# Column fixes on GpSimd, four spectra kept, and the last 16 projections written behind the second filter's forward products

## The chip, the cores and the metric

The kernel runs on one NeuronCore of a Trainium2 chip. The core has five engines that work at the same time, each through its own list of instructions in order: TensorE (matrix products, PE in the profile, with its weight loads as PEld), VectorE (DVE), ScalarE (ACT), GpSimd (POOL) and SyncE (SP), which here only issues transfers. ScalarE and GpSimd issue transfers too; all of them run on 16 DMA engines. The metric is the device time of one execution in microseconds (us), as the median of several.

## The reference

One residual layer of a sequence model, 1024 time steps by 1024 channels, in float32. After an RMS norm one projection gives 56 blocks of 128 columns: inputs and gates of a state-space branch, three inputs and a gate of a Hyena branch, and merge gates. The change touches only the Hyena branch. Cut to what matters:

```python
sc = conv_b
for j in range(3):                      # width-3 convolution in time of the projections
    sc = sc + pp[:, j:j + L] * conv_w[j]
v, x1, x2 = jnp.split(sc, 3, axis=-1)
kf = hyena_filters(...)                 # spectra of two filters, length 2L
z = v
for o, g in enumerate((x1, x2)):
    zf = jnp.fft.rfft(z, n=2 * L, axis=1)
    conv = jnp.fft.irfft(zf * kf[:, o][None], n=2 * L, axis=1)[:, :L]
    z = g * (conv + d[o] * z)
return z * jax.nn.silu(gate)
...
merged = m[..., :D] * y_s5 + m[..., D:] * (y_hy @ w_branch_hy)
out = rmsnorm(x + merged @ w_out)
```

So there are two rounds of forward transform, product with a filter's spectrum, and way back (inverse transform and gate). The second round needs the first one's result; its gate x2 times silu(gate) needs only the projections.

## The kernel before

**Projections.** `proj(c, use)` computes one block of 128 columns for all 1024 time steps: 48 products of 128x512 into a PSUM tile `pps` of two banks, in three passes of 16 (high part of the weights with the high and the low part of x, low part of the weights with the high part of x). `use` then reads the tile away. There are two `pps` tiles. A weight block is loaded by SyncE (`wraw`), ScalarE writes its high part `whi` and the negative of that into `wlo`, and a transfer issued by GpSimd adds `wraw` to `wlo` (line 512); there are two pairs of `whi` and `wlo` and three `wraw`.

**Forward transforms** (`forward`). For a group of 256 channels, products with constant matrices `zc` (3 MB in SBUF) give even parts `fwe` and odd parts `fwo` in four PSUM tiles. There are 4 groups of 4 steps each. VectorE joins even and odd parts, multiplies with the filter's spectrum `kt` (lines 718 and 719) and forms the result, which ScalarE's queue stores to memory (`d_y`). Two steps take 39 products.

**Ways back** (`inverse`). One of 8 channel blocks takes four spectra `yraw`, which ScalarE and VectorE split into high and low parts `y`, and 48 products with the constants `ic` into one PSUM tile `iv`. ScalarE copies half of it (`isn`), VectorE forms sum and difference (`pm`). In the first way back (`hy_inverse0`, `rotate`), GpSimd multiplies with the gate and writes sum and difference back into the gate's tile, and two VectorE instructions repair the first column (lines 823 and 824). Then eight transposes (`zt`) turn it, and it is stored for the second round. There are five gate tiles, three of them named `gate`, two inside `u`.

**The second forward stage** (`hy_forward1`) runs a generator of the forward steps and, in a loop over 8 blocks, two projections each: the silu gate, and x2 with its convolution and product with that gate (`fold`, lines 588 to 590: half of the product on GpSimd, half on VectorE). After each projection the loop lets some steps through, by a table:

```python
for _ in range((2, 3, 0)[(2 * c + i) % 3]):
    next(f, None)
```

After the twelfth projection it closes the stage's pools, so that the SBUF of the forward constants goes to the constants and buffers of the second way back (`inverse_tail`). That way back runs together with the first two projections of the branch's output (`w_branch_hy`); six more, and the product with `w_out`, follow.

**What sets the order.** The kernel is written in a framework that builds each engine's list ahead of the run: an instruction's place in the program is its priority, and the builder takes a later instruction first where it reckons that an earlier one must wait. It also hands out buffers, and adds the waits on semaphores. At run time each engine keeps to its list.

**Where tiles lie.** The forward constants of the second stage lie where the gate tiles lay, so their load waits for the last transposes of the first way back. The constants of the second way back lie where the second stage's buffers lay.

Of the kernel before, what the change touches and what calls it, by code (L numbers as in the profile page):

```python
# [12 lines left out]
ALU = mybir.AluOpType  # L13
# [87 lines left out]
class Trunk:  # L101
# [703 lines left out]
    def hy_inverse0(self):  # L805

        tc, nc = self.tc, self.nc
        self.d_z1 = self.dram.tile([4, 128, 2, 2048], F, name="d_z1")
        with ExitStack() as ctx:
            self.inv_pools(ctx, 0, (4, 2))  # L810
            zp = ctx.enter_context(tc.tile_pool(name="iv_z", bufs=1, side="right"))
            pi = ctx.enter_context(tc.tile_pool(name="iv_p", bufs=1, space=PSUM, side="right"))
            pt = ctx.enter_context(tc.tile_pool(name="iv_pt", bufs=2, space=PSUM, side="right"))
            gates, back = {}, {}
            self.inverse_start(0)

            def rotate(c):
                g = gates.pop(c)
                pm = self.inverse(pi)
                nc.gpsimd.tensor_tensor(out=pm, in0=pm, in1=g, op=ALU.mult)  # L820
                nc.gpsimd.tensor_tensor(out=g[:, 0], in0=pm[:, 0], in1=pm[:, 1], op=ALU.add)
                nc.gpsimd.tensor_tensor(out=g[:, 1], in0=pm[:, 0], in1=pm[:, 1], op=ALU.subtract)
                nc.vector.tensor_copy(out=g[:, 0, 0:1], in_=pm[:, 0, 0:1])
                nc.vector.tensor_scalar(out=g[:, 1, 0:1], in0=pm[:, 1, 0:1], scalar1=-1.0, scalar2=None, op0=ALU.mult)
                back[c] = g

            def store(c):
                z = zp.tile([128, 2, 8, 128], R, name="z1")
                self.to_time(pt, back.pop(c).rearrange("p a b -> p (a b)"), z)
                nc.scalar.dma_start(out=self.d_z1[c // 2][:, c % 2], in_=z.rearrange("p h a c -> p (h a c)").bitcast(F))  # L830

            for c in range(10):
                def use_x1(ps):
                    g = self.gates[c % len(self.gates)]
                    self.fold(self.conv(ps, 8 + c, "cv"), None, g)
                    gates[c] = g.rearrange("p a b c d -> p a (b c d)")

                if c < 8:
                    self.proj(16 + c, use_x1)
                if 0 < c < 9:  # L840
                    rotate(c - 1)
                if c > 1:
                    store(c - 2)

    def hy_forward1(self, tail):

        nc = self.nc
        self.d_x2 = self.dram.tile([8, 128, L], F, name="d_x2")
        with self.tc.tile_pool(name="sg", bufs=1) as sp, self.tc.tile_pool(name="vf1", bufs=2) as self.vf, \
                ExitStack() as ctx:  # L850
            wp, fwd = self.fwd_pools(ctx, 1)

            def forwards():
                for cq in range(4):
                    z = wp.tile([128, 2, 2, 8, 128], R, name="z")
                    for ct in range(2):
                        nc.sync.dma_start(out=z[:, ct].rearrange("p h a c -> p (h a c)").bitcast(F),
                                          in_=self.d_z1[cq][:, ct])
                    yield
                    yield from fwd(cq, z)  # L860

            f = forwards()
            next(f)
            for c in range(8):
                silu = sp.tile([128, L], F, name="sg")

                def use_g(ps):
                    nc.scalar.activation(out=silu, in_=ps, func=AF.Silu)

                def use_x2(ps):  # L870
                    t = self.vf.tile([128, 2, 2, 2, 128], F, name="vf")
                    self.fold(self.conv(ps, 16 + c, "cv"), silu, t)
                    nc.scalar.dma_start(out=self.d_x2[c], in_=t.rearrange("p a b c d -> p (a b c d)"))

                for i, (col, use) in enumerate(((32 + c, use_g), (24 + c, use_x2))):
                    self.proj(col, use)
                    for _ in range((2, 3, 0)[(2 * c + i) % 3]):
                        next(f, None)
                    if 2 * c + i == 11:
                        ctx.close()  # L880
                        tail()

    def exp(self, pool, out, x, shape):

# [598 lines left out]
```

## Time and profile before

| | |
|---|---|
| median of 3 runs | 1446.65 us (1445.04 to 1446.68) |
| the profiled execution | 1447.77 us |
| its span, from the first to the last instruction | 1445.9 us |
| around the span | 1.87 us |
| TensorE busy in the span | 93% |
| VectorE busy in the span | 70% |
| mean granted TensorE clock | 0.972 of 2.4 GHz |

The share of busy time is a mean over stages with different limits. A wait is worth something only where TensorE, or what it will wait for, ends last. Matmuls overlap each other, so the time of one is read from a long run of them, not from its own duration.

### The profile page before, as it was taken

The page shows a single profiled execution, that of the slowest core. Times are in us where ns is not written, and L with a number is a line of the kernel's source. Part 1 is how long each engine was busy: PE and PEld are TensorE (multiplying, and loading weights), DVE is VectorE, ACT ScalarE, POOL GpSimd, SP SyncE. Part 2 cuts the span into 40 slices and gives each one's busy share as a digit, 9 for nine tenths or more (in the row PEclk, how much of TensorE's full clock was granted, in tenths as well). Part 3 has the DMA queues.
Part 4 walks back from the last instruction along what each step waited for, and adds up shares of the span by engine and source line. Part 5 has one row for each costly group of instructions (what it writes and reads, how often), then busy time and mean ns, then how long its engine had stood idle before and what let it go on. Part 6 is the DMA issues. An engine that isn't in the chain of part 4 may idle for free.

```text
span 1445.9 us, 19569 instructions
## 1 busy us (share of the span) xinstructions
PE 1343.9 (93%) x7219; PEld 1132.4 (78%) x7219; DVE 1009.2 (70%) x1954; ACT 515.7 (36%) x737; POOL 379.6 (26%) x315
## 2 busy tenths in 40 slices
PE   5888999999999999999999999999999925999998
PEld 3776898888888887878788888888888825978886
DVE  7999997698689877224399994554379984842632
ACT  5576663223233332442322322533322213422322
POOL 3766774000000000232112100343311111432222
PEclk9998999999999999999999999999999967999999
DMA  8211225855784654667956569767788889666332
GB/s 277 90 73 73 89 110 144 199 154 140 201 264 109 139 127 84 167 159 223 315 162 172 178 175 282 195 175 200 254 265 267 268 253 306 184 175 160 119 115 73
DMA packets 188618, 257.23 MB, mean 178 GB/s; under 512 B 23069, under 2 KB 144153, under 8 KB 185788
## 3 DMA queue, kind: packets, MB, share of 16 engines
q1 hardware_dynamic: 149212, 153.69, 34.2%
q0 software_dynamic: 11520, 39.85, 14.6%
q10 hardware_dynamic: 27792, 62.45, 12.1%
q8 instruction: 57, 0.93, 0.3%
q14 instruction: 37, 0.30, 0.1%
HBM read 147.49 MB, written 76.82 MB: 155 GB/s over the span
## 4 chain that ended last, share of the span: by engine, by line
PE 66%; DVE 14%; DMA 8%; issue 2%; ACTq 0%; ACT 0%; SPq 0%; DVEq 0%
PE pps L541 42%; PE iv L634 6%; PE ops L1384 6%; DMA d_y<-x 3%; PE po L404 2%; DMA zc<-c_zc_lo_d 2%; PE fwo L685 2%; PE pe L414 1%; PE fwe L685 1%; DVE st L1216 1%; PE zt L670 1%; DVE st L1214 1%; PE s5ps L1166 1%; DVE e L338 1%; DVE m L719 1%
## 5 line engine op out<-in xcount | busy, mean ns | idle before, releaser
L512 POOL DMA_DIRECT2D wlo<-wraw x76 | 66.8, 879 | 717.8 <-ACT wlo L511 568.3
L541 PE MATMUL pps<-xh,whi 128*128 128x512 f32 x896 | 229.1, 400 | 3.2 <-DVE cv L565 3.2
L541 PE MATMUL pps<-xl,whi 128*128 128x512 f32 x896 | 224.3, 397 | 0.0
L541 PE MATMUL pps<-xh,wlo 128*128 128x512 f32 x896 | 223.9, 396 | 0.0
L541 PEld LDWEIGHTS pps<-xh,whi 128*128 128x128 f32 x896 | 165.9, 189 | 40.1 <-ACT wlo L511 3.6
L541 PEld LDWEIGHTS pps<-xh,wlo 128*128 128x128 f32 x896 | 166.5, 188 | 38.3
L541 PEld LDWEIGHTS pps<-xl,whi 128*128 128x128 f32 x896 | 166.2, 188 | 38.2 <-issue 0.2
L510 ACT CAST whi<-wraw 128x1024 fp32r<-128x1024 f32 (+1 forms) x76 | 74.7, 983 | 310.3 <-PE pps L541 267.9
L404 PE MATMUL po<-sh,fo 128*128 128x256 f32 x512 | 99.8, 289 | 6.9 <-DVE sh L111 5.7
L634 PEld LDWEIGHTS iv<-ic,y 128*128 128x128 f32 x752 | 96.3, 193 | 3.3 <-DVE y L113 0.6
L634 PE MATMUL iv<-ic,y 128*128 128x256 f32 (+1 forms) x752 | 97.7, 285 | 0.0
L113 DVE TENSOR_TENSOR y<-yraw,y 128x512 fp32r<-128x512 f32 x64 | 52.8, 837 | 55.4 <-ACT y L109 54.9
L404 PEld LDWEIGHTS po<-sh,fo 128*128 128x128 f32 x512 | 82.8, 194 | 9.8 <-DVE sh L111 6.7
L511 ACT ACTIVATE wlo<-whi 128x1024 fp32r<-128x1024 f32 (+1 forms) x76 | 74.9, 985 | 20.6 <-PE pps L541 20.4
L357 POOL TENSOR_TENSOR acc<-acc,sq 128x512 f32<-128x512 f32 x56 | 76.4, 1365 | 21.7 <-ACT sq L342 20.0
L404 PE MATMUL po<-sl,fo 128*128 128x256 f32 x256 | 73.4, 287 | 1.0 <-DVE sl L113 1.0
L109 ACT CAST y<-yraw 128x512 fp32r<-128x512 f32 x64 | 39.2, 620 | 76.2 <-PE iv L634 45.9
L563 DVE SCALAR_TENSOR_TENSOR cv<-pps,cw,cv 128x1023 f32<-128x1023 f32 x24 | 30.7, 1280 | 30.4 <-ACT cv L562 30.4
L685 PE MATMUL fwo<-z,zc 128*128 128x256 f32 x384 | 51.7, 288 | 0.0
L404 PEld LDWEIGHTS po<-sl,fo 128*128 128x128 f32 x256 | 49.5, 193 | 2.3 <-DVE sl L113 1.6
L685 PEld LDWEIGHTS fwo<-z,zc 128*128 128x128 f32 x384 | 50.1, 197 | 1.0
L333 PE MATMUL g<-w3h,ha 128*128 128x512 f32 x64 | 32.6, 510 | 18.4 <-DVE e L338 16.6
(437 smaller groups left out, 2662.4 us busy)
## 6 DMA issues: line engine op xcount, KB each, us to landing
wlo<-wraw POOLq DMA_DIRECT2D x64, 512.0 KB, 5.8
wraw<-w_in SPq DMA_DIRECT2D x56, 512.0 KB, 4.7
kspec<-ko SPq DMA_DIRECT2D x32, 512.0 KB, 3.0
kt<-kspec SPq DMA_DIRECT2D x32, 512.0 KB, 5.4
d_y<-x ACTq DMA_DIRECT2D x32, 512.0 KB, 3.9
yraw<-d_y SPq DMA_DIRECT2D x64, 256.0 KB, 4.9
d_m<-cv ACTq DMA_DIRECT2D x16, 512.0 KB, 2.7
d_z<-z ACTq DMA_DIRECT2D x8, 1024.0 KB, 6.1
```

The source lines that it names most:

```text
L109: nc.scalar.copy(out=hi, in_=src)
L113: e.tensor_tensor(out=lo, in0=src, in1=hi, op=ALU.subtract)
L333: nc.tensor.matmul(out=ps, lhsT=ha[:, tsl], rhs=w3h, start=True, stop=False)
L357: nc.gpsimd.tensor_tensor(out=acc, in0=acc, in1=sq, op=ALU.add)
L404: nc.tensor.matmul(out=po[:, part], lhsT=fo[a][:, 12 * (jj % 2) + b], rhs=sd[4 + i][d][:, part], start=n == 0 and part == 0, stop=n == 11 ...
L510: nc.scalar.copy(out=hi, in_=raw)
L511: nc.scalar.activation(out=lo, in_=hi, func=AF.Copy, scale=-1.0)
L512: nc.gpsimd.dma_start(out=lo, in_=raw, accum_op=ALU.add)
L541: nc.tensor.matmul(out=ps[:, hf * 512:hf * 512 + 512], lhsT=w[:, kc], rhs=part(x, kc, hf), start=a == 0 and p == 0 and kc == 0, stop=b == ...
L634: nc.tensor.matmul(out=dst, lhsT=lhsT, rhs=self.ic[b][:, j, cols], start=first, stop=last)
L685: nc.tensor.matmul(out=out, lhsT=zc[a][:, b], rhs=z[:, :, d, zi], start=start and n == 0, stop=stop and n == 3 * len(prods) - 1)
L1384: nc.tensor.matmul(out=pss[cs.start][:, 0:cs.stop - cs.start], lhsT=m[:, kc, ts], rhs=w[kc][:, cs], start=kc == 0 and p == 0, stop=kc == 7 ...
```

## The change

Three things change. In the first way back, buffers for four split spectra `y` are kept instead of two, and as many are prepared ahead. The two column repairs of each channel go from VectorE to GpSimd, behind GpSimd's own three instructions. In the second forward stage, the program writes out all 16 steps first, closes the stage's pools and opens those of the second way back, and only then writes the 16 projections. These then have a lower priority than the forward steps, and the builder decides where they go.

```diff
@@ hy_inverse0
-            self.inv_pools(ctx, 0, (4, 2))
+            self.inv_pools(ctx, 0, (4, 4))
...
                 nc.gpsimd.tensor_tensor(out=g[:, 1], in0=pm[:, 0], in1=pm[:, 1], op=ALU.subtract)
-                nc.vector.tensor_copy(out=g[:, 0, 0:1], in_=pm[:, 0, 0:1])
-                nc.vector.tensor_scalar(out=g[:, 1, 0:1], in0=pm[:, 1, 0:1], scalar1=-1.0, scalar2=None, op0=ALU.mult)
+                nc.gpsimd.tensor_copy(out=g[:, 0, 0:1], in_=pm[:, 0, 0:1])
+                nc.gpsimd.tensor_scalar(out=g[:, 1, 0:1], in0=pm[:, 1, 0:1], scalar1=-1.0, scalar2=None, op0=ALU.mult)
@@ hy_forward1
-            f = forwards()
-            next(f)
+            for _ in forwards():
+                pass
+            ctx.close()
+            tail()
             for c in range(8):
...
-                for i, (col, use) in enumerate(((32 + c, use_g), (24 + c, use_x2))):
+                for col, use in ((32 + c, use_g), (24 + c, use_x2)):
                     self.proj(col, use)
-                    for _ in range((2, 3, 0)[(2 * c + i) % 3]):
-                        next(f, None)
-                    if 2 * c + i == 11:
-                        ctx.close()
-                        tail()
```

How the lists move, at three places. First TensorE, from the last forward products of the second stage (`fwo`) to the first product of the second way back (`iv`). Before:

```order
L685 MATMUL fwo<-z,zc_8981 128x256 x2
L685 MATMUL fwo<-z,zc_8982 128x256
L541 MATMUL pps<-xl,whi 128x512 x10
L541 MATMUL pps<-xh,wlo 128x512 x16
L632 MATMUL iv<-icp,y 128x512
```

With the change:

```order
L685 MATMUL fwo<-z,zc_8982 128x256
L541 MATMUL pps<-xl,whi 128x512 x10
L541 MATMUL pps<-xh,wlo 128x512 x16
L541 MATMUL pps<-xh,whi 128x512 x16
L541 MATMUL pps<-xl,whi 128x512 x16
...
L632 MATMUL iv<-icp,y 128x512
```

Where 26 projection products stood between the last forward product and the first inverse one, 202 stand now (in the rows left out the rest of this projection, two whole ones, and 32 products of the last).

Second TensorE, at the end of the first way back: its last inverse products (`iv`), the last channels' transposes (`zt`), and the first forward products (`fwe`, `fwo`, whose operands `zc_8981` and `zc_8982` are the high and the low constants). Before:

```order
L634 MATMUL iv<-ic_7644,y 128x256
L541 MATMUL pps<-xh,whi 128x512 x12
L541 MATMUL pps<-xl,whi 128x512 x16
L541 MATMUL pps<-xh,wlo 128x512 x16
L541 MATMUL pps<-xh,whi 128x512 x4
L670 MATMUL zt<-ident,gate_6581 128x128 x4
...
L541 MATMUL pps<-xl,whi 128x512 x16
L541 MATMUL pps<-xh,wlo 128x512 x16
L541 MATMUL pps<-xh,whi 128x512 x3
L685 MATMUL fwe<-z,zc_8981 128x256 x4
```

With the change:

```order
L634 MATMUL iv<-ic_7644,y 128x256
L670 MATMUL zt<-ident,gate_6580 128x128 x8
L541 MATMUL pps<-xl,whi 128x512 x8
L541 MATMUL pps<-xh,wlo 128x512 x16
L670 MATMUL zt<-ident,gate_6581 128x128 x8
L685 MATMUL fwe<-z,zc_8981 128x256 x4
L685 MATMUL fwo<-z,zc_8981 128x256 x4
L685 MATMUL fwe<-z,zc_8982 128x256
```

Before, 48 projection products stand ahead of the last channel's transposes and 47 among and behind them; now 24 ahead and none behind, until the forward products that need the new constants.

Third GpSimd, at the first channels of the first way back, with the change (before, lines 823 and 824 are not in this list, and each weight's transfer, line 512, stands between two channels):

```order
L820 TENSOR_TENSOR pm<-pm,gate_6579 128x1024
L821 TENSOR_TENSOR gate_6579<-pm 128x512
L822 TENSOR_TENSOR gate_6579<-pm 128x512
L823 COPY gate_6579<-pm 128x1
L824 TENSOR_SCALAR gate_6579<-pm 128x1
L512 DMA wlo<-wraw 128x1024
L820 TENSOR_TENSOR pm<-pm,gate_6580 128x1024
```

Each channel has five GpSimd instructions now instead of three.

## Rows read from the trace of the kernel before

**Rows 1.** The page: span, and busy tenths and granted clock in 40 slices.

```profile
span 1445.9 us, 19569 instructions
...
PE   5888999999999999999999999999999925999998
...
PEclk9998999999999999999999999999999967999999
```

**Rows 2.** Stretches: length, busy us of each engine, clock, DMA share, GB/s.

```profile
core 0: us, PE busy (x) PEld busy (x) DVE busy (x) ACT busy (x) POOL busy (x), PEclk, DMA share, GB/s
893.03:1025.16 132.13, 132.13 (x781) 116.06 (x780) 63.08 (x111) 56.27 (x78) 48.90 (x32) 1.00 0.71 193
...
1038.02:1055.07 17.05, 14.45 (x66) 11.47 (x65) 5.24 (x7) 3.87 (x5) 3.95 (x3) 1.00 0.98 320
1055.07:1160.60 105.53, 105.25 (x599) 91.69 (x600) 96.50 (x126) 23.31 (x26) 12.61 (x9) 1.00 0.81 260
1160.60:1166.66 6.06, 6.05 (x26) 4.53 (x25) 5.88 (x10) 1.05 (x1) 0.00 (x0) 1.00 0.91 264
1166.66:1208.72 42.06, 0.00 (x0) 0.00 (x0) 21.40 (x27) 4.87 (x5) 4.71 (x3) 0.53 0.92 290
1208.72:1216.84 8.12, 8.12 (x47) 7.89 (x48) 4.14 (x6) 3.10 (x5) 0.00 (x0) 0.68 1.13 327
```

**Rows 3.** Whom TensorE waited for, 890 to 1300: total, times, longest.

```profile
PE iv L632 <- DMA yraw<-d_y: 42.1, 1, 42.1
PE fwe L685 <- DMA zc<-c_zc_lo_d: 2.6, 1, 2.6
...
PE fwe L685 <- DMA z<-d_z: 0.3, 1, 0.3
```

**Rows 4.** Timeline, last forward product to first inverse product.

```profile
1159.00 1.60 PE L685 MATMUL fwo<-z,zc 128*128 128x256 f32 x12
...
1186.26 1.22 DVE L719 TENSOR_TENSOR m<-x,kt 128x1024 f32<-128x1024 f32 x1
...
1187.50 0.32 SPq L596 DMA_DIRECT2D icp<-c_ic_d  x1
...
1208.72 0.79 PE L632 MATMUL iv<-icp,y 128*128 128x512 f32 x1 [42.07 <-DMA yraw<-d_y]
```

**Rows 5.** Whom SyncE waited for, 1020 to 1210.

```profile
SPq L508 <- DMA wlo<-wraw: 83.3, 10, 14.4
...
SPq L596 <- DVE m L719: 3.9, 1, 3.9
```

**Rows 6.** The chain that ended last: start, us, what.

```profile
1016.43 2.76 PE iv L634 x23
...
1063.62 2.88 PE fwo L685 x24
...
1282.00 67.44 PE pps L541 x288
```

**Rows 7.** Groups by form: GpSimd in the whole run, VectorE and GpSimd from 893.03 to 1033.

```profile
L162 POOL MEMSET raw<- 128x128 f32 x1 | 0.2, 204 | 0.3 <-POOLq L1472 0.3
...
L820 POOL TENSOR_TENSOR pm<-pm,gate 128x1024 f32<-128x1024 f32 x6 | 14.4, 2404 | 30.4 <-DVE pm L643 26.2 <-DVE vf L590 4.2
L822 POOL TENSOR_TENSOR gate<-pm 128x512 f32<-128x512 f32 x6 | 7.8, 1296 | 0.0
...
L823 DVE COPY gate<-pm 128x1 f32<-128x1 f32 x6 | 0.9, 154 | 20.7 <-POOL gate L821 20.7
```

**Rows 8.** Timeline, end of the first way back: last gate, transposes, load.

```profile
1032.72 0.15 DVE L824 TENSOR_SCALAR gate<-pm 128x1 f32<-128x1 f32 x1 [1.10 <-POOL gate L822]
...
1037.40 0.60 PE L670 MATMUL zt<-ident,gate 128*128 128x128 f32 x4
...
1038.02 0.32 SPq L660 DMA_DIRECT2D zc<-c_zc_hi_d  x1
```

**Rows 9.** VectorE's groups by form, 1055.07 to 1190.05.

```profile
L719 DVE TENSOR_TENSOR m<-x,kt 128x1024 f32<-128x1024 f32 x16 | 23.3, 1458 | 0.0
...
L718 DVE TENSOR_TENSOR m<-x,kt 128x1024 f32<-128x1024 f32 x16 | 19.5, 1220 | 0.3
...
L565 DVE SCALAR_TENSOR_TENSOR cv<-pps,cw,cv 128x1023 f32<-128x1023 f32 x4 | 5.1, 1278 | 0.0
...
L589 DVE TENSOR_TENSOR vf<-cv,sg 128x512 f32<-128x512 f32 x4 | 4.7, 1186 | 0.0
```

**Rows 10.** Stretches after the wait, columns as in rows 2.

```profile
1212.00:1214.00 2.00, 2.00 (x11) 2.00 (x11) 0.69 (x1) 0.61 (x1) 0.00 (x0) 0.53 1.05 364
1214.00:1216.00 2.00, 2.00 (x19) 2.00 (x18) 0.69 (x1) 0.62 (x1) 0.00 (x0) 1.00 1.07 358
```

## The prediction

> **What bounds the kernel now.** I read the page first: TensorE is busy nearly everywhere, in tenths of forty slices, except in two slices late in the span, where the granted clock falls too [rows 1]. A table by stretches then cuts that part at the stages the change touches [rows 2]. The first way back (893.03 to 1025.16) has TensorE busy all the time. From the last product of the second forward stage TensorE still has 6 us of projection and then does nothing for 42.06 us (1166.66 to 1208.72); this is its one long wait there [rows 3], and in it the clock drops to half. The timeline shows why: the last forward product ends at 1160.6, VectorE's last use of a filter spectrum (L719) at 1187.48, and only then can SyncE issue the constants of the second way back, which take the forward stage's SBUF; the spectra's loads come behind them and the first inverse matmul starts at 1208.72 [rows 4]. SyncE's waits confirm the releaser, a VectorE multiplication (L719) [rows 5]. So at this place neither TensorE nor its projections bound the kernel, but a chain VectorE, constants, spectra, with no TensorE work left under it.
>
> The second forward stage itself is VectorE's: of the 105.5 us in which TensorE computes it, VectorE is busy 96.5 [rows 2]. From the landing of its constants (1055.07) to the issue at 1187.50 it takes 132.4 us for 16 steps, 8.3 us each.
>
> **What the change does to TensorE's list.** All 16 projections of the last loop have lower priority than the 16 forward steps. By the order of the built program, the first way back now takes 216 projection matmuls instead of 340 before its last inverse matmul, since with four spectra kept a channel's 48 matmuls stand in one piece; 24 more precede the forward stage; 310 stand between the first and the last forward product, and 218 behind it, of which 202 ahead of the second way back (before: 26, all ahead). No matmul is added or removed. So the question is only how much TensorE waits between 893 and 1209.
>
> **Prices.** A projection matmul takes 67.44/288 = 0.234 us, an inverse one 2.76/23 = 0.12, a forward one 2.88/24 = 0.12 [rows 6]. A channel of the way back is 48 x 0.12 = 5.8 us plus about 0.9 for its eight transposes (two pieces of 0.60 [rows 8] that overlap their neighbours). Check on before: 340 x 0.2335 + 8 x 5.8 + 7 x 0.9 = 132.1, the stretch measured 132.13.
>
> **First way back.** 216 x 0.2335 + 8 x 5.8 + 6 x 0.9 = 102.2 us, so the last inverse matmul would end at 995.2 without waits. There is one PSUM tile for the inverse, so the next channel waits for ScalarE's copy and VectorE's subtraction. Between channels there are 24 to 36 projection matmuls (5.6 to 8.4 us), except once, where five stand (1.2 us plus transposes): about 1 us of wait. VectorE and ScalarE have room there: 63 and 56 us busy of 132, with the old pace [rows 2]. I put 1.5 us, between 0 and 6 (one more such wait of some 0.75 us per channel). End: 996.7.
>
> **Column fixes.** Two one-column VectorE instructions of 0.15 us each leave a channel, and two on GpSimd come [rows 7]. The trace has no GpSimd instruction of one column. From below the nearest is a fill of 128x128 at 0.2 us, from above the 128x512 addition at 1.30 [rows 7]; it is a dispatch with almost no data, so 0.2, together 0.4 a channel. A channel's GpSimd work is then 2.4 + 1.3 + 1.3 + 0.4 = 5.4 us every 7 to 15 us, and the transposes that want it stand a channel later, under projections. Only the last channel shows it. VectorE no longer waits in line for GpSimd (20.7 us at L823 for six channels [rows 7]); at this place that was not TensorE's wait, and brings nothing by itself.
>
> **The new wait.** The forward constants lie where the gates lay, so their load starts when the last channel's transposes have read its gate. Before, the gate was ready 7.7 us after the last inverse matmul (1025.16 to 1032.87), the transposes stood later in the list, and the load was issued at 1038.02 [rows 8]; its second half landed at 1055.07, 17.05 us later. Then projections covered nearly all of it. Now the list has only transposes (0.9) and 24 projection matmuls (5.6), then the last transposes, then forward products. Gate ready at 7.7 + 0.4, a GpSimd DMA issue ahead of it at most 0.9, transposes 0.9: the load starts 9.5 us after the last inverse matmul (8.7 to 12.9 + 2.6), at 1006.2, and lands 17 us later, at 1023.3. TensorE waits 9.5 + 17.05 - 6.5 - 0.9 - 1.0 = 18.2 us (1.0 for the eight products that need the first half alone, which stand inside the wait).
>
> **Forward stage and after.** It starts at 1023.3 instead of 1055.07, 31.8 us earlier. VectorE has the same 16 steps, four x2 channels as before, and two folds left over from the way back, 2 x 1.2 [rows 9]: 134.8 us. Its path: 1023.3 + 134.8 + 21.2 (issue to first inverse matmul, from 1187.50 to 1208.72) = 1179.3. TensorE's path: 528 projection matmuls (123.3) and 304 products (36.5), 159.8 us, plus waits. Products wait for VectorE to free one of four PSUM tiles. Up to the last product TensorE has 310 x 0.2335 + 36.5 = 109 us of work; VectorE lags the last product by 27 us (1160.6 to 1187.5), so it allows that product at 134.8 - 27 = 108. The two are about equal, which means small waits wherever the mixture is uneven: the first two groups of 39 products stand with no projection between them (about 3 us), later ones 1 to 3 us. I put 8, between 1 and 20. TensorE is through its projections at 1023.3 + 159.8 + 8 = 1191.1, against 1208.72 before: 17.6 us earlier, and 8 us behind the constants, so that wait is gone.
>
> **Clock.** After the long wait TensorE ran at half speed (1.2 GHz of 2.4) until about 1214 [rows 10]; its first 47 inverse matmuls took 8.12 us instead of 5.8 [rows 2]. These 2.3 us come back, as the inverse now follows projections. The new wait has a slow spell of its own, but in products that VectorE paces; I leave it in the 8 us. Against the 2.3 stands x2's last channel, whose VectorE work (two of 1.28 and one of 1.2 [rows 9]) now falls into the second way back: 0 to 4 us, I take 2.
>
> **Sum.** 17.6 + 2.3 - 2 = 17.9 us less. The profiled execution took 1447.77 (span 1445.9 and 1.87 around it); 1429.9. It lies 1.1 above the median shown, so 1429 as a median. Counted by waits: 42.06 + 2.9 [rows 3] + 2.3 go, 1.5 + 18.2 + 8 + 2 come, 17.6.
>
> **Rivals.**
> - The mixture in the forward stage is bad and TensorE waits for VectorE step by step. For it: VectorE is the stage's bound, and 218 projection matmuls now stand behind the last product, so a delay of that product is paid in full. Against: TensorE has work for 109 us where VectorE allows 108, and the price of 8 already holds the last product at 117. At 5 us more wait it is 1434. If a step costs s more than 8.3, the last product can't come before 108 + 16 s; from s = 1.7 (10 us a step) the whole gain of 18 is gone, and at s = 2.2 the time is 1429 + 108 + 35 - 117 = 1455, slower. What speaks for longer steps: a VectorE multiplication that meets GpSimd's fold is stretched (mean of L719 1.46 us, of its twin L718 1.22 [rows 9]), and two more folds come into the stage; but that is a few us in all, not 2 a step.
> - The constants are late again: SyncE works in line, and a weight load ahead of them waits for an accumulating transfer (83.3 us of such waits in ten cases, up to 14.4 [rows 5]). If one of 14.4 stood right there, 1179.3 becomes 1193.7, where TensorE arrives at 1191.1 - 16 x 0.234 = 1187.4: it waits 6.3 us, 1435.
> - The new wait is shorter. The transfer engines moved 320 GB/s in those 17.05 us [rows 2], 5.5 MB, of which the constants are 3.1; alone they would take 9.8 us, and the time would be 1422. The 2 MB of inputs and 1 MB of filter spectra that are issued just ahead of them speak against it.
> - No interleaving at all. The Trainium skill, Perfetto Trace Analysis, section Optimization Strategy, advises to interleave regimes that different engines bound, and the change removes the interleaving that was written out by hand. What that would do here, from rows: VectorE's stage ends at 1023.3 + 134.8, and the 123.3 us of projections follow it, 21.2 of them under the loads; the way back would then be held until 1281 instead of 1208.7, and the time would be about 1520. The order speaks against it: 310 projection matmuls stay among the products.
>
> **Chances.** The forecast (a gain of 9 to 27 us) 0.70; the bad mixture 0.14 (0.05 of it still faster, 0.04 no change, 0.05 slower); late constants 0.06; the shorter wait 0.08; no interleaving 0.02. Range 1416 to 1441: below, the waits of the forward stage at 1 and a load of 12 us; above, 20 us of them. About 0.2% (2.9 us) is what a measurement tells from no change: faster 0.89, same 0.04, slower 0.07.
>
> **What would show it.** The last inverse matmul of the first way back ends near 997; TensorE then waits some 19 us, in pieces, for the gate and the forward constants; these land near 1023; no wait over 3 us stands ahead of the second way back, which starts near 1188; GpSimd's fixes take 0.1 to 0.3 us. Wrong if the forward stage, from the constants' landing to its last product, takes over 125 us, or the first way back over 110.

## The result, and the profile after

The changed kernel takes 1428.21 us (median of 4 runs, 1425.86 to 1432.84) against 1446.66 before; the ratio is 0.9878, with a 95% interval of 0.985 to 0.9905. That is 18.5 us less, where 1429 was predicted (1416 to 1441). The profiled execution took 1429.32 us. Its page:

```profile
span 1427.5 us, 19583 instructions
...
PE   5888999999999999999999999999599998999997
...
PEclk9999999999999999999999999999799999999999
```

The long hole of [rows 1] late in the span has become a short one at slice 29, where the first way back gives over to the second forward stage. The totals from the first inverse matmul of the first way back to the end, first of before and then of after (columns as in [rows 2]):

```profile
894.66:1445.90 551.24, 497.76 (x2699) 426.28 (x2697) 313.46 (x470) 170.63 (x242) 142.97 (x88) 0.96 0.67 201
```

```profile
894.74:1427.50 532.76, 500.22 (x2689) 426.43 (x2687) 316.95 (x452) 167.94 (x239) 148.83 (x104) 0.97 0.68 207
```

TensorE's idle time fell from 53.5 to 32.5 us, and its busy time rose by 2.5, in stretches at the half clock. The same part by stretches, of after:

```profile
894.74:994.85 100.11, 98.77 (x635) 88.94 (x634) 50.30 (x85) 41.78 (x62) 42.16 (x40) 1.00 0.68 194
994.85:1005.89 11.04, 8.40 (x40) 6.17 (x38) 2.61 (x6) 3.67 (x5) 6.23 (x6) 0.91 0.90 312
1005.89:1021.06 15.17, 2.05 (x8) 1.78 (x8) 1.77 (x3) 1.07 (x2) 0.61 (x1) 0.50 1.02 383
1021.06:1133.85 112.79, 111.23 (x615) 95.91 (x616) 102.81 (x131) 25.14 (x28) 16.37 (x11) 0.99 0.75 243
1133.85:1157.26 23.41, 23.41 (x102) 18.81 (x102) 23.08 (x31) 6.35 (x6) 7.49 (x3) 1.00 0.69 195
1157.26:1183.69 26.43, 23.72 (x103) 18.76 (x101) 8.14 (x9) 6.68 (x8) 4.17 (x3) 1.00 1.07 332
1183.69:1187.79 4.10, 3.98 (x18) 3.67 (x19) 2.87 (x5) 2.13 (x4) 0.61 (x1) 0.62 1.06 366
```

From the top: the first way back, 30 us shorter than before; the last gate; the load of the forward constants, with TensorE nearly idle; the forward products to the last one; from there to the issue of the constants of the second way back; projections over that load; and the first 18 inverse matmuls of the second way back. TensorE's waits from 885 to 1300 (compare [rows 3]; lines after the edit are three lower than before):

```profile
PE fwe L685 <- issue: 10.2, 1, 10.2
PE fwe L685 <- DMA zc<-c_zc_lo_d: 3.0, 1, 3.0
PE iv L632 <- ACT y L109: 2.7, 1, 2.7
PE zt L670 <- POOL gate L823: 2.1, 1, 2.1
PE fwe L685 <- DVE x L715: 1.5, 2, 0.8
PE iv L632 <- DVE pm L642: 1.4, 1, 1.4
PE iv L632 <- ACT cv L562: 1.3, 1, 1.3
PE iv L634 <- DVE y L113: 1.3, 3, 0.7
```

The wait of 42.1 us for the spectra is gone; the new one stands in four pieces (L685 twice, L670 twice, 15.8 us with a last 0.5). Where it comes from is in the timeline of the changed kernel, at the place that [rows 8] showed of before:

```profile
1003.19 0.19 POOL L823 COPY gate<-pm 128x1 f32<-128x1 f32 x1
1003.43 0.82 PE L670 MATMUL zt<-ident,gate 128*128 128x128 f32 x4 [2.12 <-POOL gate L823]
1004.14 0.52 POOL L824 TENSOR_SCALAR gate<-pm 128x1 f32<-128x1 f32 x1
1004.72 1.11 PE L670 MATMUL zt<-ident,gate 128*128 128x128 f32 x4 [0.46 <-POOL gate L824]
1005.89 0.32 SPq L660 DMA_DIRECT2D zc<-c_zc_hi_d  x1
1016.05 1.19 PE L685 MATMUL fwe<-z,zc 128*128 128x256 f32 x4 [10.23 <-issue]
1021.06 1.43 PE L685 MATMUL fwe<-z,zc 128*128 128x256 f32 x5 [2.96 <-DMA zc<-c_zc_lo_d]
```

The fixes on GpSimd (0.19 us, and 0.52 where GpSimd issues a DMA in between), the last transposes, the issue of the constants, the first eight products with their first half, and the rest 15.2 us after the issue. Over the way back the groups of the two fixes, answering to [rows 7], have means of 0.34 and 0.43 us, pulled up by such cases:

```profile
L824 POOL TENSOR_SCALAR gate<-pm 128x1 f32<-128x1 f32 x6 | 2.6, 426 | 0.0
L823 POOL COPY gate<-pm 128x1 f32<-128x1 f32 x6 | 2.0, 341 | 0.0
```

### The profile page after: what moved, and what is told of

Same layout as the page of the kernel before. It is cut to its first block, busy times and chain, and to the rows that moved or that the text cites. A ratio compares the mean times of both kernels' runs of the same rounds, so it can differ in the third digit from the quotient of the medians.

```text
span 1427.5 us, 19583 instructions
## 1 busy us (share of the span) xinstructions
PE 1348.4 (94%) x7219; PEld 1134.9 (80%) x7219; DVE 1014.9 (71%) x1938; ACT 515.0 (36%) x737; POOL 383.6 (27%) x331
## 4 chain that ended last, share of the span: by engine, by line
PE 61%; DVE 17%; DMA 8%; issue 3%; ACT 1%; SPq 1%; ACTq 0%; POOL 0%; DVEq 0%
PE pps L541 39%; PE ops L1381 6%; PE iv L634 4%; PE po L404 2%; DMA zc<-c_zc_lo_d 2%; DMA d_y<-x 2%; PE fwo L685 2%; DMA yraw<-d_y 2%; PE pe L414 1%; DVE m L719 1%; PE fwe L685 1%; DVE st L1213 1%; DVE st L1211 1%; DVE e L338 1%; PE zt L670 1%
## 5 line engine op out<-in xcount | busy, mean ns | idle before, releaser
L113 DVE TENSOR_TENSOR y<-yraw,y 128x512 fp32r<-128x512 f32 x64 | 58.1, 926 | 65.6 <-ACT y L109 65.5
L685 PE MATMUL fwo<-z,zc 128*128 128x256 f32 x384 | 50.7, 285 | 0.0
L685 PEld LDWEIGHTS fwo<-z,zc 128*128 128x128 f32 x384 | 49.1, 194 | 1.3 <-issue 0.4
```

Of the source, the lines that this page charges most:

```text
L113: e.tensor_tensor(out=lo, in0=src, in1=hi, op=ALU.subtract)
L685: nc.tensor.matmul(out=out, lhsT=zc[a][:, b], rhs=z[:, :, d, zi], start=start and n == 0, stop=stop and n == 3 * len(prods) - 1)
```

## The experiments

Each kernel is compared with runs of the kernel before on the same chip, whose median was 1446.7 us for after, 1446.4 for spectra_only, fixes_only, eight_kb and three_raw, 1445.9 for the temps_first group and vector_more, and 1444.3 for the others. "After" is the changed kernel, and after_again the same kernel measured once more. The marks are from each profiled execution, counted from its own first inverse matmul of the first way back: the issue of the forward constants, the start of the unbroken forward products, the issue of the constants of the second way back, its first matmul, and the end.

```
                         us       ratio (95%)              zc    prod.  ic    back2  end
before                   -        1                        143.4 160.4 292.8 314.1 551.2
after                    1428.2   0.9878 (0.985-0.9905)    111.2 126.3 262.5 289.0 532.8
after_again              1429.1   0.9893 (0.9877-0.9909)   110.7 126.2 263.1 289.6 532.4
spectra_only             1429.4   0.9878 (0.9858-0.9898)   109.4 126.3 261.9 288.6 531.0
fixes_only               1441.3   0.9967 (0.9954-0.998)    144.1 161.4 288.4 308.7 547.0
eight_kb                 1435.2   0.9922 (0.9904-0.9941)   125.1 142.3 271.3 293.2 538.2
three_raw                1435.9   0.9927 (0.9909-0.9944)   126.3 144.7 273.1 296.8 540.3
temps_first              1430.9   0.9894 (0.9877-0.9912)   100.1 123.4 268.7 289.1 534.3
temps_first_three_raw    1435.7   0.9932 (0.992-0.9945)    109.9 135.7 286.7 296.8 539.7
temps_first_two_raw      1430.5   0.9896 (0.9882-0.991)    106.3 133.0 284.0 292.0 533.9
vector_more              1438.2   0.9951 (0.9937-0.9965)   110.8 126.1 272.4 295.8 540.9
vector_less              1429.7   0.99 (0.9886-0.9914)     111.2 126.1 258.8 287.7 531.8
gates_on_u               1427.3   0.9877 (0.986-0.9893)    100.2 121.7 259.9 286.5 529.3
gates_on_u_gpsimd        1430.1   0.9902 (0.9886-0.9919)   100.2 121.4 264.0 290.3 534.9
```

**Which part is it?** The part of the diff that looks largest, the last 16 projections written behind the forward steps, does nothing alone: in the program built from before with this edit the lists of all five engines are those of before, row for row. It was therefore not run. The other two parts were.

```diff
-            self.inv_pools(ctx, 0, (4, 2))
+            self.inv_pools(ctx, 0, (4, 4))
```

> The kernel before with one edit: four split spectra are kept in the first way back instead of two. Column fixes stay on VectorE and the last loop stays as it was written. By its built program TensorE's list is that of the changed kernel but for some 25 of 3,100 rows: about 200 projection matmuls in the first way back, 24 between it and the forward stage, 201 behind the last forward product. Theory: the order on TensorE is all that the change is worth, and it comes from the kept spectra; 1428 us (1425 to 1432). Rival: it takes the last 16 projections standing behind the forward steps in the program, or GpSimd's column fixes; then at least 9 of the 18 us are missing, 1437 or more.

It measured 1429.4 us with the ratio of the whole change, and its marks are those of after within 1.8 us. The kept spectra alone bring all that can be measured, with the old last loop and with the fixes on VectorE.

```diff
-                nc.vector.tensor_copy(out=g[:, 0, 0:1], in_=pm[:, 0, 0:1])
-                nc.vector.tensor_scalar(out=g[:, 1, 0:1], in0=pm[:, 1, 0:1], scalar1=-1.0, scalar2=None, op0=ALU.mult)
+                nc.gpsimd.tensor_copy(out=g[:, 0, 0:1], in_=pm[:, 0, 0:1])
+                nc.gpsimd.tensor_scalar(out=g[:, 1, 0:1], in0=pm[:, 1, 0:1], scalar1=-1.0, scalar2=None, op0=ALU.mult)
```

> The kernel before with one edit: the two column fixes on GpSimd. Its list on TensorE stays that of before in what counts: about 334 projection matmuls in the first way back, 98 between it and the forward stage, 19 behind the last forward product. Theory: the fixes are worth nothing by themselves, 1446.7 us (1444 to 1449), with a wait of some 40 us ahead of the second way back. Rival: VectorE's 20.7 us of waiting for GpSimd in the way back [rows 7] held something back; then the way back is shorter and the time is 1441 or less.

1441.3 us: alone the fixes bring 5 us, near the rival's figure, but not at the rival's place. The constants are issued no earlier (144.1 against 143.4), and the wait ahead of the second way back stands:

```profile
PE iv L632 <- ACT y L109: 39.3, 1, 39.3
```

The 5 us arise in the forward stage (from the products to the next constants 127.0 us instead of 132.4), where VectorE's waits for the store of an earlier spectrum (`x` has three buffers) are fewer; the kernel before first, then this one:

```profile
L714 DVE TENSOR_TENSOR x<-ke,fwo 128x512 f32<-128x512 f32 x16 | 11.0, 685 | 8.0 <-DMA d_y<-x 8.0
```

```profile
L714 DVE TENSOR_TENSOR x<-ke,fwo 128x512 f32<-128x512 f32 x16 | 10.9, 681 | 2.1 <-DMA d_y<-x 1.2 <-PE fwo L685 0.7
```

The edit gives the scheduler other readiness times, and it fills in projections elsewhere; that this other mixture shortens the waits is read from the rows, not tested. Beside the kept spectra the fixes bring nothing that can be measured (after_again 0.9893, spectra_only 0.9878).

**The spectra, or the room they take?** Two more split spectra take 8 KB a partition. So to the kernel before a tile of that size is added, which lives through the way back and holds nothing of use:

```diff
+            pad = ctx.enter_context(tc.tile_pool(name="iv_pad", bufs=1, side="right")).tile([128, 2048], F, name="pad")
...
+                if c in (0, 7):
+                    nc.gpsimd.tensor_copy(out=pad[:, 0:1], in_=z[:, 0, 0, 0:1].bitcast(F))
```

> The kernel before (two spectra kept, fixes on VectorE, the old program order), with a tile of 8 KB a partition that lives through the first way back and does nothing, apart from two one-column copies into it. That is the SBUF that two more spectra take. In the built program the tiles of the x2 fold then find no room until the way back is over, as in the changed kernel: 234 projection matmuls in the way back, none between it and the forward stage, 199 behind the last forward product. Theory: SBUF is what moves the projections. The last inverse matmul would end at 894.7 + 234 x 0.2335 + 51.9 = 1001, with a few waits 1003; the constants land some 26 us behind it (as in the changed kernel), 1029, and the way back starts 162 us later, at 1191 against 1183.7; 1435 us (1429 to 1441). Rival: the gain comes from the four spectra, which keep a channel's 48 inverse matmuls in one piece; then this kernel is at 1446 or, with more waits, above.

1435.2 us, where 1435 was expected: a dead tile alone brings 11 us, where the whole change brings 18. And the reverse, the changed kernel with its four spectra and 2 KB less beside them:

```diff
-            self.inv_pools(ctx, 0, (4, 4))
+            self.inv_pools(ctx, 0, (3, 4))
```

> The changed kernel with three buffers for the spectra as loaded instead of four, 2 KB a partition less. In the built program the x2 folds then find their room during the way back: it keeps 217 projection matmuls, but 110 instead of 24 stand between it and the forward stage, and 121 instead of 202 behind the last forward product. So the new wait of 15.8 us is covered, and the cover of the later wait is cut by 19 us. Theory (the landing of the forward constants and VectorE's chain behind it set the second way back): the constants land near 1029 instead of 1021, the way back starts 154 to 162 us later, 1183 to 1191, with no projection left over, and TensorE waits 15 to 25 us ahead of it; 1426 us (1421 to 1431). Rival (TensorE's list is the bound, and the new wait is paid in full): 1428 - 13 = 1415.

1435.9 us: above the range of the theory, and far from the rival. What room does is seen in GpSimd's part of the x2 fold (L588). Its first rows in the timelines of before, after, eight_kb and three_raw:

```profile
939.71 2.53 POOL L588 TENSOR_TENSOR vf<-cv,sg 128x512 f32<-128x512 f32 x1 [9.01 <-DVE cv L565]
971.88 2.21 POOL L588 TENSOR_TENSOR vf<-cv,sg 128x512 f32<-128x512 f32 x1 [0.61 <-DVE cv L565]
```

```profile
1020.45 2.13 POOL L588 TENSOR_TENSOR vf<-cv,sg 128x512 f32<-128x512 f32 x1 [15.79 <-DMA d_z<-z]
```

```profile
1022.27 2.11 POOL L588 TENSOR_TENSOR vf<-cv,sg 128x512 f32<-128x512 f32 x1
```

```profile
945.86 2.15 POOL L588 TENSOR_TENSOR vf<-cv,sg 128x512 f32<-128x512 f32 x1
991.07 2.15 POOL L588 TENSOR_TENSOR vf<-cv,sg 128x512 f32<-128x512 f32 x1
```

In after the fold's tile `vf` waits for the store of the way back's last tile `z1` (L830), since it lies where the way back's tiles lay: by the built programs the two `vf` tiles take bytes 96064 to 104256 of a partition, and the lowest tile of the way back begins at 110496 in before, at 102304 in after and with the dead tile, and at 104352 in three_raw. Without a fold the gate `sg` and the two PSUM tiles of the projections stay taken (its second SiLU, L870, runs at 1028.43, its first at 908.20), and the last loop stops after its first columns. These projections, put off, are what lets the way back end early. In three_raw the folds run in the way back, 110 projection matmuls stand behind it, and the new wait is covered but for 4.5 us; but the transposes of the last gate stand behind 59 projection matmuls, the constants come 15 us later than in after, and the cover is missing at the other end:

```profile
PE iv L632 <- DMA yraw<-d_y: 19.5, 1, 19.5
```

So kept spectra and missing room can each do the work of the other. Between the first and the last inverse matmul of the first way back stand 335 projection matmuls in before, 234 with the dead tile alone, 217 in three_raw, which keeps four split spectra and lets the folds run (with one loaded spectrum less, and with the other two edits), and 200 in after. Each alone brings 10 to 11 us, both together 18.

The Trainium skill (Perfetto Trace Analysis, section Optimization Strategy) says that repeated gaps can mean too little SBUF or PSUM for the next tile. What the trace shows here is a single gap of such a cause, and on GpSimd, its wait of 15.8 us for a store. It cuts the other way: too little room held work back that was better done later.

**What sets the second way back?** The changed kernel with one VectorE addition more in each forward step, then with one less:

```diff
+                if o:
+                    nc.vector.tensor_tensor(out=x[:, 0:2], in0=m[:, 0, :, 0], in1=m[:, 0, :, 1], op=ALU.add)
```

> The changed kernel with one more VectorE addition of 128x512 in each of the 16 forward steps of the second forward stage; its result is written over by the next instruction, so the output is unchanged. An addition of this size has a place of 0.61 us in VectorE's row; 16 of them are 9.8 us. The built program answers with 335 projection matmuls among the products and 193 behind them. Theory (VectorE's chain sets the second way back): the last spectrum and the loads behind it come 9.8 us later, near 1193, with no projection left over (3.7 us): 1434 us (1431 to 1438). Rival (TensorE's list is the bound, VectorE has room): 1428 to 1430.

1438.2 us, 9 to 10 more than the changed kernel's two medians: from the products to the next constants it takes 146.3 us instead of 136.2, with VectorE busy for 135.3 of them instead of 125.9. That is a little above the theory's range; VectorE had no room.

```diff
-                nc.vector.tensor_tensor(out=y[:, 1], in0=m[:, :, 0, 0], in1=m[:, :, 1, 0], op=ALU.subtract)
+                if o == 0:
+                    nc.vector.tensor_tensor(out=y[:, 1], in0=m[:, :, 0, 0], in1=m[:, :, 1, 0], op=ALU.subtract)
```

> The changed kernel without one subtraction of 128x512 on VectorE in each of the 16 steps of the second forward stage (the second half of each spectrum is left as it was, so its values are not the reference's): 9.8 us less on VectorE. Theory (VectorE's chain and TensorE's list end within some 3 us of each other in the changed kernel): the constants of the second way back are issued 9.8 us earlier, but TensorE is through the projections ahead of it only at 1181; it loses the wait of 2.7 us, the slow spell behind it and some small waits: 1423 us (1420 to 1425). First rival (VectorE's chain alone): 1418.5. Second rival (VectorE has room): 1428.

1429.7 us, nothing gained, as the second rival had it, but not for its reason: with vector_more VectorE has no room. Of the 9.8 us only 3.5 reach the issue of the constants (132.7 us after the products instead of 136.2), since TensorE's last product still comes 112.0 us after the start (112.8 in after), and VectorE's idle time up to that issue grows from 10.3 to 16.5 us. Of the 3.5 another 2.4 go at the next step (28.9 us from the issue to the first matmul instead of 26.5), where SyncE holds the last part of these constants for the store of an x2 channel:

```profile
SPq L599 <- DMA d_x<-vf: 10.1, 1, 10.1
```

TensorE is through the projections ahead of the second way back at 286.8 us, counted as the marks are (286.2 in after). So TensorE's list, VectorE's chain and the last x2 store end close together: more of one costs in full, less of one brings nothing.

**The new wait.** The following edits of the changed kernel bring its load forward. The first lets the work tiles of the forward stage, which no load fills, take the gates' room:

```diff
-        cp, wp, tp = mk("fw_c", 1), mk("fw_w", 1), mk("fw_t", 3)
+        if o:
+            tp, cp, wp = mk("fw_t", 3), mk("fw_c", 1), mk("fw_w", 1)
...
```

> The changed kernel with one edit: in the second forward stage the pool of work tiles that no load fills is laid out first, so that it and not the forward constants takes the SBUF of the gates. The constants then wait for the last inverse matmul of the first way back (994.9) and no more for the transposes of the last gate (1005.3). In the built program 247 projection matmuls instead of 310 stand among the forward products, and 265 instead of 202 behind them. Theory (the landing of what the forward products need, and VectorE's chain of 136 us behind it, set the second way back): the constants are issued near 995, the inputs behind them, the products start at 1009 to 1013 instead of 1021, the way back some 10 us earlier, 1418.5 us (1415 to 1422). Rival (TensorE's list is the bound from the constants on): it takes 160 us of matmuls plus some 14 us of waits, since 94 us of work now stand where VectorE needs 108; it is through its projections at 1188 against 1191.9, 1425 us or more.

1430.9 us. The constants were issued 11 us earlier, as expected, but now the inputs `z` waited for the transposes instead:

```profile
994.96 0.34 SPq L660 DMA_DIRECT2D zc<-c_zc_hi_d  x1
...
1004.77 0.88 SPq L860 DMA_DIRECT2D z<-d_z  x2
...
1018.24 2.26 PE L685 MATMUL fwe<-z,zc 128*128 128x256 f32 x9 [12.33 <-DMA d_z<-z]
```

The products start 3 us earlier, and the new layout delays the constants of the second way back by 6. The time is on the rival's side. The wait was moved, not removed, and with 265 projection matmuls behind the products TensorE comes to the second way back without a wait, so its list ends last there, as the rival had it. With fewer buffers for the spectra as loaded, in two sizes:

```diff
-            self.inv_pools(ctx, 0, (4, 4))
+            self.inv_pools(ctx, 0, (3, 4))
```

> The edit of temps_first and that of three_raw together: the forward constants are loaded without waiting for the last gate, and 104 projection matmuls stand between the way back and the forward stage, which is so covered. In the built program 309 stand among the products and 122 behind them. Theory (landing and VectorE's chain): the constants are there in time, the products start when TensorE comes to them, near 1032 (1005.7, the end of the way back in three_raw, and 104 x 0.2335 + 2), 8.6 us ahead of three_raw's; 1435.9 - 8.6 = 1427 us (1423 to 1431), above temps_first, with a wait of 15 to 25 us ahead of the second way back. Rival (TensorE's list is the bound, and each wait that is covered is a gain): with no wait ahead of the forward stage it beats temps_first, 1417 or less.

> As temps_first_three_raw, with two buffers for the spectra as loaded: 203 projection matmuls in the way back, 104 between it and the forward stage, 297 among the products, 148 behind them. Theory (landing and VectorE's chain): the products start near 1027, the second way back near 1181 behind a wait of 5 to 13 us; 1424 us (1420 to 1428). Rival (TensorE's list): 1417 or less, as its sister.

(The second has (2, 4).) 1435.7 and 1430.5 us, both above the theory's range and 13 us or more above the rival's. The products start without a wait, at 135.7 and 133.0, and a wait of 21.8 and 15.9 us stands ahead of the second way back. The next test moves the last two gates out of the pool, and nothing else:

```diff
+                    self.gates = [self.gates[i] for i in (0, 3, 4, 1, 2)]
```

> The changed kernel with the five gate tiles in another order, so that the last two channels' gates lie in the two tiles that stand outside the gates' pool. Nothing else moves: TensorE's list has the same 200, 24, 310 and 202 projection matmuls. The forward constants then wait only for the last inverse matmul of the first way back (994.9) and no more for the last transposes (1005.3). They are issued with the inputs and the filter spectra, 6.2 MB at some 390 GB/s, 16 us: the products start near 1012 instead of 1021. Theory (the start of the products sets all that follows, and the new wait is paid in full when the load itself comes earlier, not when projections are put under it): 9 us less, 1419 us (1416 to 1422). Rival (the loads share one rate, so that an earlier issue lands hardly earlier, as in temps_first): 1425 us or more.

1427.3 us, far from the theory's 1419; the fastest median, but against after_again (1429.1) inside the noise. The constants are issued 11 us earlier in this kernel, and the products start 4.6 us earlier, not 9. Inputs and constants now share one rate from the issue to the start:

```profile
997.52:1019.09 21.57, 7.71 (x40) 5.83 (x39) 4.31 (x9) 4.73 (x7) 6.23 (x6) 0.77 0.96 348
```

The estimate of 390 GB/s is near the rate in the wait of after (383); from this issue to the start it is 348, over 7.5 MB. Of the 4.6 us some 3 are left at the end of the span by the marks, which are of one execution each. The time is on the rival's side; whether anything was gained, the times can't tell.

```diff
+                    self.gates = [self.gates[i] for i in (0, 3, 4, 1, 2)]
...
-                nc.vector.tensor_tensor(out=y[:, 1], in0=m[:, :, 0, 0], in1=m[:, :, 1, 0], op=ALU.subtract)
+                (nc.gpsimd if o else nc.vector).tensor_tensor(out=y[:, 1], in0=m[:, :, 0, 0], in1=m[:, :, 1, 0], op=ALU.subtract)
```

> The edit of gates_on_u, and the last subtraction of each of the 16 steps of the second forward stage moved from VectorE to GpSimd (the 128x512 subtraction takes GpSimd 1.27 us, VectorE 0.61 of its row). Theory: VectorE's chain is up to 9.8 us shorter, less what GpSimd's share stretches (0.24 us where two meet, some 4 us in all); TensorE's list leaves 3 to 5 us of it: 1415 us (1411 to 1419) where gates_on_u has 1419. Rival (the spectra are stored later and each buffer comes free later, since GpSimd is slower): 1420 us or more.

1430.1 us, the rival's side. VectorE is rid of 16 subtractions, but waits longer for stores (10.4 us against 7.7 in gates_on_u) and 5.6 us for ScalarE, and more of its instructions are stretched; these are its groups over the forward stage, in this kernel:

```profile
L719 DVE TENSOR_TENSOR m<-x,kt 128x1024 f32<-128x1024 f32 x16 | 25.3, 1582 | 0.0
...
L714 DVE TENSOR_TENSOR x<-ke,fwo 128x512 f32<-128x512 f32 x16 | 11.0, 686 | 10.4 <-DMA d_y<-x 10.4
```

## Why the prediction was right

The forecast of 1429 us stands at 1428.2, and its chain was the right one: a way back that ends 30 us earlier, constants that land earlier, VectorE's chain behind them, no long wait ahead of the second way back. By its own steps:

- **First way back.** 216 projection matmuls, the end at 996.7 with 1.5 us of waits: measured 994.85, with 1.3 us of waits. The 1.9 us are the start: 16 of the 216 run from 891.00, ahead of the first inverse matmul, and the prediction counted all of them from 893.03.
- **Why 216.** The prediction read the number off the built program and gave two reasons, the lower priority of the last projections and the spectra that keep a channel in one piece. The first is wrong: that part alone moves no row of the built lists, and spectra_only, with the old last loop, has 200 between the first and the last inverse matmul as after has. The second is some of it (three_raw, with a channel in one piece and the folds in the way back, has 217 and is at 1435.9). What the prediction lacked is SBUF: the x2 folds find no room until the way back is over. eight_kb shows what that does alone, with 234. The forecast did not suffer, since it took the order from the built program.
- **Column fixes.** 0.2 us each on GpSimd: 0.19 to 0.21 alone, 0.34 and 0.43 on average, a little over the 0.1 to 0.3 that was to be seen; the last channel shows 0.19 and 0.52, the second with a DMA issue in between. "Brings nothing by itself" holds beside the spectra; in the kernel before, alone, they bring 5 us through another mixture.
- **The new wait.** 18.2 us: measured 15.8 (2.1 + 0.5 + 10.2 + 3.0). The issue comes 11.0 us after the last inverse matmul and not 9.5, and the load takes 15.2 us and not 17.05, at 383 GB/s instead of 320; together 26.2 where 26.55 was forecast. The rest is no gain: TensorE's own pieces in it take 10.45 us instead of 8.4, with the clock at 0.91 and then 0.50. The third rival, constants alone in 9.8 us, did not come.
- **Forward stage.** The start at 1023.3 was 1021.06; the last product 117 us behind it was 112.8, because the 8 us for waits and the slow spell were 3.8, of which 1.5 are waits. Of the prediction's terms this one was 4.2 us too large. The two limits, 109 for TensorE and 108 for VectorE, were called about equal, and vector_more and vector_less agree with that. VectorE's path of 134.8 us was 136.2, no sign of the first rival.
- **The second way back.** It was to start near 1187.4 with no wait over 3 us: 1183.69, with 2.7. From the issue to the first matmul it took 26.4 us instead of 21.2, the term that was 5.2 us too small, and TensorE's projections were done 2.7 us ahead of it. The last of this was ScalarE's list:

```profile
1180.22 1.05 ACT L510 CAST whi<-wraw 128x1024 fp32r<-128x1024 f32 x1 [15.71 <-DMA yraw<-d_y]
1181.17 1.02 ACT L870 ACTIVATE sg<-pps 128x1024 f32<-128x1024 f32 x1
1182.09 1.05 ACT L511 ACTIVATE wlo<-whi 128x1024 fp32r<-128x1024 f32 x1
1183.03 2.17 ACT L109 CAST y<-yraw 128x512 fp32r<-128x512 f32 x4
1183.69 0.49 PE L632 MATMUL iv<-icp,y 128*128 128x512 f32 x1 [2.71 <-ACT y L109]
```

ScalarE's wait for a spectrum's load ends at 1180.2, and a weight's two casts and a SiLU stand ahead of the first split. vector_less, gates_on_u and spectra_only have the same order there; what moving the split ahead would bring was not tested. SyncE held the first of these constants for VectorE's last multiplication alone, so the second rival did not come.

- **Clock and x2.** The 2.3 us of slow matmuls did not come back: after the short wait the first 18 inverse matmuls took 4.10 us instead of 2.2. In the second way back stand another 2.7 us of waits for split spectra and for VectorE's reading of PSUM (1.3 and 1.4). From its start to the end it takes 243.8 us; the prediction had 240.6 (1429.9 - 1.9 - 1187.4).

The start came 3.7 us earlier than predicted and the rest was 3.2 us longer: the forecast hit the time because two terms of that size were off in opposite directions. The mechanism was foreseen; that the time agrees to 1 us is luck. The fourth rival, no interleaving, did not come: 310 projection matmuls stay among the products.

Why the stall ahead of the second way back was worth 18 us and not 42 is seen in three_raw and the temps_first pair: projections that cover the new wait are missing ahead of the second way back, where a wait of 16 to 22 us returns. There is only so much work to put under two waits.

## What to carry to other kernels

When a scheduler fills gaps with independent work, a larger buffer count can act through the room it takes as well as through the buffers: build a version with a dead tile of the same size before you credit the buffers. Covering a wait with work that is also the only cover of a later wait gained nothing in any of three kernels here. An earlier issue counts only as far as the load lands earlier: 11 us earlier brought the products 4.6 us earlier here, and nothing that the times can tell. Where two engines' limits and a buffer's release end within a few us of each other, test with more work as well as with less: less alone would have said that VectorE has room.

## What the runs showed of the hardware

A wait of 2.7 us, after a stretch in which TensorE was busy throughout (the clock 1.00), was followed by half the clock. In the timeline by 2 us, of after:

```profile
1183.00:1185.00 2.00, 1.20 (x5) 0.88 (x6) 1.33 (x3) 2.00 (x5) 0.87 (x1) 0.93 1.03 409
1185.00:1187.00 2.00, 2.00 (x11) 2.00 (x11) 1.17 (x2) 0.45 (x2) 0.00 (x0) 0.50 1.05 381
```

The matmuls that followed the wait ran at 1.2 GHz, the lower level, about 2 us more than the same work takes at 2.4. One-column instructions on GpSimd cost as little as 0.19 us, no more than its fill of 128x128 in [rows 7]. And the mean of 1.46 us of VectorE's multiplication of 128x1024 (L719), where its twin L718 takes 1.22, hides two sorts. In the changed kernel 14 of the 16 take 1.2 us and two take 3.15 and 3.18; each of the two starts within 1 us of a fold's multiplication on GpSimd (L588). At a third meeting the fold was stretched instead:

```profile
1029.54 2.23 POOL L588 TENSOR_TENSOR vf<-cv,sg 128x512 f32<-128x512 f32 x1 [6.96 <-ACT sg L870]
1029.69 3.15 DVE L719 TENSOR_TENSOR m<-x,kt 128x1024 f32<-128x1024 f32 x1
...
1147.10 5.82 POOL L588 TENSOR_TENSOR vf<-cv,sg 128x512 f32<-128x512 f32 x1 [3.83 <-issue]
1148.01 1.21 DVE L719 TENSOR_TENSOR m<-x,kt 128x1024 f32<-128x1024 f32 x1
```

In gates_on_u_gpsimd the mean is 1.58 because three meet a fold (3.16 us each), not by the subtractions that GpSimd has there in each step.
